# The first matrix of an MLP by Strassen's scheme, its results through DRAM

## The chip, the cores and the metric

The kernel is one program on one core of a Trainium2 chip. The metric is the device time of one execution in microseconds (us). Engines are called as in the profile: PE (TensorE, the matrix multiplier), DVE (VectorE), ACT (ScalarE), POOL (GpSimd) and SP (SyncE, which issues the DMAs here). A matrix product accumulates in a PSUM bank; a bank holds 128 x 512 values of 32 bits, and there are eight, called bank0 to bank7.

## The reference

Two blocks of a network run one after the other on 1024 tokens of 1024 channels. The change touches the last stage, the MLP of the second block, whose hidden layer is 4096 wide:

```python
def squared_relu_mlp(x, w1, w2):
    hdn = jnp.square(jax.nn.relu(jnp.einsum('bld,df->blf', x, w1.astype(jnp.float32))))
    return jnp.einsum('blf,fd->bld', hdn, w2.astype(jnp.float32))
...
        h = layer_norm_2(ALPHA * h + cross_attention(...), ln2_g[l], ln2_b[l])
        h = layer_norm_2(ALPHA * h + squared_relu_mlp(h, mlp_w1[l], mlp_w2[l]), ln3_g[l], ln3_b[l])
```

Everything is in fp32. `layer_norm_2` subtracts the mean of a token's channels and divides by the root of their variance (plus 1e-5), then applies a gain and a bias.

## The kernel before, in words

P is 128, D and T (channels and tokens) are 1024, HALF is 512, KD is 8. Channels lie on the partitions: the activations are held per half of the tokens (`self.h[hf]`, hf 0 or 1) as 128 x 8 x 512, part k being channels 128k to 128k+127.

**Products of fp32 matrices.** The matmuls take operands of type fp32r, and every operand x is split into two of them: hi, x cast to fp32r, and lo, x - hi. `split` (L165) does that with a cast on ACT (L166) and a subtraction on DVE (L167); `wload` (L139) loads a block of weights of 128 x 1024 into a tile `wraw` and splits it likewise into `whi` (ACT, L149) and `wlo` (DVE, L150). `mm3` (L153) then issues three matmuls for each 128 x 128 piece of weights and 512 tokens: hi x hi (L157), hi x lo (L158), lo x hi (L159). So a product over all 1024 channels takes 8 x 3 = 24 matmuls into one bank.

**The MLP.** `mlp` (L1904) goes through the hidden layer in eight steps, fb = 0 to 7, of 512 hidden channels. In a step, the first matrix runs over four weight blocks of 128 hidden channels, each times two halves of the tokens: eight groups of 24 matmuls, the activations (`act[hf]`, tiles ahi and alo of each half) being the moving operand. The sink of each group applies ReLU from the bank (ACT, L1914), squares it (DVE, L1915), and splits the result into a pair of x4 tiles, the operand `fa` of the second matrix. Then four blocks of the second matrix run, each as four groups of 12 matmuls, and each group is added to `h` (L1935 in step 0, L1937 after). The last step ends in `mlp_last` (L1939), which computes the last part of the second matrix with the operands exchanged, a token block at a time, normalizes and stores it. In step 0 the first matrix goes through `gemm_lag`, which starts a block's first half of the tokens two blocks ahead of its second half, because the second half of the activations comes later: it is the normalization of `norm_ln` (L1857 to L1860), in front of the MLP.

**What sets the order.** The kernel is written as a plain sequence; a tile scheduler orders each engine's instructions by a simulated timeline and by priorities. `early(...)` raises the priority of what is issued in it, as the weight loads and the sinks are. Within an engine instructions run in the order that came out, and each waits for the semaphores of what it reads or overwrites. SP issues the DMAs in the same way. Tiles come from pools with a fixed number of buffers to a tag: three each for wraw, whi and wlo (L1057), four each for x40 and x41, seven for x2, three each for y20 and y21 (L1802 to L1810). A tile of a tag can only be written when the tile that had its buffer has been read for the last time. PSUM banks are dealt in rings (L95): mm is banks 0 and 1.

## Time and profile before

| what | value |
|---|---|
| time, median of 3 runs | 3163.79 us (3158.67 to 3164.6) |
| profiled execution, its own time | 3173.28 us |
| span of that execution | 3171.5 us |
| mean granted clock of PE | 0.964 |
| PE busy | 97% of the span, 15504 matmuls |
| weight loads of PE (PEld) busy | 79% |
| DVE busy | 59% |
| ACT busy | 30% |
| POOL busy | 9% |

The span runs from the first to the last instruction of the profiled execution; its own time holds a little more around it. Durations that the trace gives are those of this one execution. Matmuls are pipelined: their recorded durations overlap, so what one costs PE is the distance of the starts of two in a row. The granted clock is the share of full clock at which PE was allowed to run: 1.00 is 2.4 GHz, 0.50 is 1.2 GHz. The MLP runs from about 2424 us (first matmuls of step 0) to the end at 3171.5.

### The profile page before, as it was taken

What the parts mean: (1) busy time and instruction counts of PE and PEld (TensorE: products, weight loads), DVE (VectorE), ACT (ScalarE), POOL (GpSimd) and SP (SyncE); (2) the same over time, 40 slices, a digit from 0 to 9 for tenths busy, and PEclk for the clock granted to TensorE, in tenths of its full rate; (3) what the DMA queues carried; (4) which work ended last, traced back from release to release, by engine and by line L of the source; (5) the groups of instructions that cost most, each with busy time, mean ns of one, the idle gap of its engine ahead of it and who ended that gap; (6) DMA issues with size and microseconds to landing.
All of it is one profiled execution on the core that took longest, in us unless ns stands there. A gap on an engine that the chain in (4) does not pass through costs nothing.

```text
span 3171.5 us, 40262 instructions
## 1 busy us (share of the span) xinstructions
PE 3061.3 (97%) x15504; PEld 2521.2 (79%) x15504; DVE 1871.1 (59%) x3884; ACT 955.0 (30%) x1650; POOL 273.0 (9%) x761
## 2 busy tenths in 40 slices
PE   8999899999989999999999899889999999999998
PEld 7978788787867887878788787778787888888887
DVE  4987657564856455564665679886456333333336
ACT  3323434343432121221243235433334111222212
POOL 0000222221085000000000000210000000000000
PEclk8999889887999999999999999999999999999999
DMA  4123444435422111121211543423021111111111
GB/s 158 52 95 107 146 109 126 114 85 155 144 64 61 51 47 57 51 61 47 73 55 47 147 137 100 127 70 110 37 87 50 54 54 47 47 47 47 47 47 54
DMA packets 193137, 254.62 MB, mean 80 GB/s; under 512 B 45745, under 2 KB 136753, under 8 KB 192433
## 3 DMA queue, kind: packets, MB, share of 16 engines
q1 hardware_dynamic: 192944, 252.05, 26.0%
q8 instruction: 122, 2.00, 0.3%
q14 instruction: 71, 0.57, 0.1%
HBM read 195.11 MB, written 57.93 MB: 80 GB/s over the span
## 4 chain that ended last, share of the span: by engine, by line
PE 84%; DVE 6%; DMA 4%; POOL 3%; issue 1%; ACT 1%; SPq 0%; ACTq 0%; DVEq 0%; POOLq 0%
PE bank L157 22%; PE bank L159 22%; PE bank L158 22%; PE bank L161 2%; PE bank L162 2%; PE bank L163 2%; PE bank L751 1%; PE bank L752 1%; DVE zt L1348 1%; PE bank L197 1%; PE bank L322 1%; DMA ix<-scr 1%; DMA zx<-zt 1%; PE bank L775 1%; PE bank L588 1%
## 5 line engine op out<-in xcount | busy, mean ns | idle before, releaser
L157 PE MATMUL bank<-ahi,whi 128*128 128x512 f32 x1856 | 743.2, 401 | 13.0 <-DVE zt L1288 4.7
L159 PE MATMUL bank<-ahi,wlo 128*128 128x512 f32 x1856 | 740.4, 399 | 0.0
L158 PE MATMUL bank<-alo,whi 128*128 128x512 f32 x1856 | 737.8, 398 | 1.1 <-DVE alo L167 1.1
L149 ACT CAST whi<-wraw 128x1024 fp32r<-128x1024 f32 (+1 forms) x242 | 253.6, 1049 | 842.9 <-PE bank L158 759.0
L157 PEld LDWEIGHTS bank<-ahi,whi 128*128 128x128 f32 x1856 | 351.3, 189 | 93.0 <-issue 6.3
L159 PEld LDWEIGHTS bank<-ahi,wlo 128*128 128x128 f32 x1856 | 354.5, 191 | 86.4 <-issue 2.1
L158 PEld LDWEIGHTS bank<-alo,whi 128*128 128x128 f32 x1856 | 351.1, 189 | 87.7 <-issue 2.7
L150 DVE TENSOR_TENSOR wlo<-wraw,whi 128x1024 fp32r<-128x1024 f32 (+1 forms) x242 | 297.3, 1229 | 166.6 <-ACT whi L149 153.4
L159 PE MATMUL bank<-x,wlo 128*128 128x512 f32 x448 | 177.9, 397 | 0.0
L158 PE MATMUL bank<-x,whi 128*128 128x512 f32 x448 | 177.1, 395 | 0.0
L157 PE MATMUL bank<-x,whi 128*128 128x512 f32 x448 | 175.4, 392 | 0.0
L1937 DVE TENSOR_TENSOR h<-h,bank 128x512 f32<-128x512 f32 x96 | 66.0, 688 | 161.0 <-PE bank L159 160.3
L157 PE MATMUL bank<-fhi,whi 128*128 128x512 f32 x352 | 139.6, 397 | 10.0 <-DVE h L1159 10.0
L158 PE MATMUL bank<-flo,whi 128*128 128x512 f32 x352 | 140.0, 398 | 0.0
L157 PE MATMUL bank<-hi,whi 128*128 128x512 f32 x320 | 130.0, 407 | 10.1 <-ACT hi L272 9.2
L159 PE MATMUL bank<-fhi,wlo 128*128 128x512 f32 x352 | 139.7, 399 | 0.0
L1159 DVE TENSOR_TENSOR h<-h,bank 128x512 f32<-128x512 f32 x96 | 65.5, 686 | 114.0 <-PE bank L159 113.9
L159 PE MATMUL bank<-hi,wlo 128*128 128x512 f32 x320 | 131.2, 410 | 0.0
L158 PE MATMUL bank<-lo,whi 128*128 128x512 f32 x320 | 130.3, 407 | 0.0
L1915 DVE TENSOR_TENSOR y<-y 128x512 f32<-128x512 f32 x64 | 44.0, 689 | 103.5 <-ACT y L1914 103.5
L157 PEld LDWEIGHTS bank<-x,whi 128*128 128x128 f32 x448 | 84.8, 189 | 19.9
L158 PEld LDWEIGHTS bank<-x,whi 128*128 128x128 f32 x448 | 84.1, 188 | 20.6
(766 smaller groups left out, 5539.8 us busy)
## 6 DMA issues: line engine op xcount, KB each, us to landing
wraw<-in_w_m_dram SPq DMA_DIRECT2D x60, 512.0 KB, 3.6
wraw<-in_w_o_dram SPq DMA_DIRECT2D x24, 512.0 KB, 4.2
wraw<-in_w_fg_dram SPq DMA_DIRECT2D x22, 512.0 KB, 3.5
wraw<-in_w_fu_dram SPq DMA_DIRECT2D x22, 512.0 KB, 3.6
wraw<-in_w_fd_dram SPq DMA_DIRECT2D x22, 512.0 KB, 3.5
hd<-h SPq DMA_DIRECT2D x4, 2048.0 KB, 6.8
s5m<-s5m SPq DMA_DIRECT2D x8, 896.0 KB, 4.7
x<-in_xT_dram SPq DMA_DIRECT2D x8, 512.0 KB, 10.1
```

The source lines that it names most:

```text
L149: nc.scalar.copy(hi[:, :n], raw[:, :n])
L150: nc.vector.tensor_sub(lo[:, :n], raw[:, :n], hi[:, :n].bitcast(F32))
L157: mm(ps, lhsT=wh, rhs=xh, start=first, stop=False)
L158: mm(ps, lhsT=wh, rhs=xl, start=False, stop=False)
L159: mm(ps, lhsT=wl, rhs=xh, start=False, stop=last)
L161: mm(ps, lhsT=xh, rhs=wh, start=first, stop=False)
L162: mm(ps, lhsT=xh, rhs=wl, start=False, stop=False)
L163: mm(ps, lhsT=xl, rhs=wh, start=False, stop=last)
L197: self.nc.tensor.matmul(ps[:, i:i + 1], lhsT=x[:, i * P:(i + 1) * P], rhs=self.k("ones")[:, 0:1], start=j == 0, stop=j == len(xs) - 1)
L1159: V.tensor_add(h, h, ps)
L1915: V.tensor_mul(x, x, x)
L1937: V.tensor_add(self.h[hf][:, d], self.h[hf][:, d], ps)
```

## The change

**What it computes.** The last 28 of the 32 weight blocks of the first matrix are taken in 14 pairs (n, n+1). Halves of channels (K, parts 0 to 3 and 4 to 7) are called L and R. With A11 = W[n] L, A12 = W[n] R, A21 = W[n+1] L, A22 = W[n+1] R, and for the activations B11, B21 = parts 0 to 3 and 4 to 7 of the first half of the tokens, B12, B22 = those of the second half, the four results of a pair (two blocks, two halves of tokens) come from seven products over half the channels each, in the Winograd form of Strassen's scheme. The order is: 1 (A11 with B11), 6 (A21 + A22 - A11 with t2), 5 (A21 + A22 with t1), 7 (A11 - A21 with t3), 2 (A12 with B21), 3 (A12 - (A21 + A22 - A11) with B22), 4 (A22 with t4), where t1 = B12 - B11, t2 = B22 - t1, t3 = B22 - B12 and t4 = B21 - t2. In the code u = t2 is computed as v + B11 with v = t3 and t4 as B21 - B11 - t3, the same sums. Each product is 4 parts x 3 = 12 matmuls into one bank (ring "fast", six banks).

**Operands** (`fast_operands`). The sums of the activations are formed once, from the fp32 values in `h`, on DVE (L1920, L1922, L1923) and POOL, and split. t2 and t3 fill all eight x4 tiles, t4 lies in six x2 tiles and two tiles of another pool, and t1 overwrites parts 0 to 3 of `act[1]`, that is B12, which no product uses by itself.

**Weights** (`fast_pairs`). A generator loads both raw blocks of a pair, forms the sums of its halves on POOL (four additions of 128 x 512 a pair) and splits each of the seven left operands into one of six slots (halves of the three whi and three wlo tiles). Six are made ahead; each product then takes the next one and asks for one more.

**Results.** ACT copies the first product out of its bank (m1), DVE adds the others as they come (L1990 to L2011, seven additions a pair), ReLU and square follow as before, and each 128 x 512 result is sent to a DRAM scratch tensor `fd[n]` (2 MB a step of four blocks). The first four blocks run as before through `gemm_lag` with their 24 matmuls and go to `fd` too. After all of the first matrix, the second matrix runs through its eight steps: each loads its four blocks from `fd` into the x4 tiles (now as raw fp32) and splits them into `act[fb % 2]`, which is no longer needed for the activations; the matmuls, the additions to `h` and `mlp_last` are as before.

```diff
--- before.py
+++ after.py
@@ -93,7 +93,7 @@
 
 
     RINGS = {"mm": "01", "l1": "4567", "s": "23", "cf": "45", "ar": "23", "ad": "4", "inv": "56", "cr": "7", "cd": "1", "ho": "2", "kv": "0", "kv0": "017", "wo": "04",
-             "s5": "34567", "s5m": "67", "dn": "0145", "ml": "234567", "rg": "2", "sa": "34", "sb": "562", "so": "7", "sc": "0123", "tp": "67"}
+             "s5": "34567", "s5m": "67", "dn": "0145", "ml": "234567", "rg": "2", "sa": "34", "sb": "562", "so": "7", "sc": "0123", "tp": "67", "fast": "234567"}
 
     def psum(self, kind):
         banks = self.RINGS[kind]
@@ -1901,23 +1901,136 @@
                         self.split(ah[:, 4:8, ls], al[:, 4:8, ls], pt)
         self.gemm_lag(self.vwd, self.act, self.ln_sink("ln2_g", "ln2_b"), 5, 3)
 
+    def fast_operands(self):
+
+        V, G = self.nc.vector, self.nc.gpsimd
+
+        def halves(tiles):
+            return [v[:, o:o + HALF] for v in tiles for o in (0, HALF)]
+        t2, t3 = ([halves([self.x4(z) for _ in range(2)]) for z in range(2)] for _ in range(2))
+        t4 = [[self.x2(dt=F32R) for _ in range(3)] + [self.t(self.rp, [P, HALF], f"rb{z}", F32R)] for z in range(2)]
+        h0, h1 = self.h
+        b11, b21, t1, b22 = ([[self.act[hf][z][:, o + k] for k in range(4)] for z in range(2)] for hf in range(2) for o in (0, 4))
+
+        for k in range(4):
+            v, u, w = (self.y2(1) for _ in range(3))
+            V.tensor_sub(v, h1[:, 4 + k], h1[:, k])
+            G.tensor_tensor(u, v, h0[:, k], op=ALU.add)
+            V.tensor_sub(w, h0[:, 4 + k], h0[:, k])
+            V.tensor_sub(w, w, v)
+            for t, x in ((t3, v), (t2, u), (t4, w)):
+                self.split(t[0][k], t[1][k], x)
+        for k in range(4):
+            u = self.y2(1)
+            G.tensor_tensor(u, h1[:, k], h0[:, k], op=ALU.subtract)
+            self.split(t1[0][k], t1[1][k], u)
+        return {1: b11, 2: b21, 3: b22, 4: t4, 5: t1, 6: t2, 7: t3}
+
+    def fast_pairs(self, srcs, ops, sink):
+
+        nc = self.nc
+        V, A, G = nc.vector, nc.scalar, nc.gpsimd
+        his, los = ([self.t(self.wp, [P, 1056], z, F32R) for _ in range(3)] for z in ("whi", "wlo"))
+        slots = [(his[j][:, o:o + HALF], los[j][:, o:o + HALF]) for j in range(3) for o in (0, HALF)]
+        at = [0]
+
+        def part(x):
+            s = slots[at[0] % 6]
+            at[0] += 1
+            self.split(s[0], s[1], x)
+            return s
+
+        L, R = slice(0, HALF), slice(HALF, 2 * HALF)
+
+        def weights():
+
+            for n in range(0, len(srcs), 2):
+                r0, r1, s = (self.t(self.wp, [P, 1056], "wraw") for _ in range(3))
+                for r, src in ((r0, srcs[n]), (r1, srcs[n + 1])):
+                    nc.sync.dma_start(r[:, :D], src)
+                yield part(r0[:, L])
+                G.tensor_tensor(s[:, L], r1[:, L], r1[:, R], op=ALU.add)
+                G.tensor_tensor(s[:, R], s[:, L], r0[:, L], op=ALU.subtract)
+                yield part(s[:, R])
+                yield part(s[:, L])
+                G.tensor_tensor(r1[:, L], r0[:, L], r1[:, L], op=ALU.subtract)
+                yield part(r1[:, L])
+                yield part(r0[:, R])
+                G.tensor_tensor(r0[:, R], r0[:, R], s[:, R], op=ALU.subtract)
+                yield part(r0[:, R])
+                yield part(r1[:, R])
+        made, todo = weights(), []
+
+        def more():
+            with self.early():
+                w = next(made, None)
+            if w:
+                todo.append(w)
+        for _ in range(6):
+            more()
+
+        def prod(m):
+            ps = self.psum("fast")
+            wh, wl = (v.rearrange("p (k n) -> p k n", k=4) for v in todo.pop(0))
+            for k in range(4):
+                self.mm3(ps, wh[:, k], wl[:, k], ops[m][0][k], ops[m][1][k], k == 0, k == 3)
+            more()
+            return ps
+        for n in range(0, len(srcs), 2):
+            p = prod(1)
+            with self.early(100000):
+                m1 = self.y2(0)
+                A.copy(m1, p)
+            p = prod(6)
+            with self.early(100000):
+                u = self.y2(1)
+                V.tensor_add(u, m1, p)
+            p5 = prod(5)
+            with self.early(100000):
+                v = self.y2(1)
+                V.tensor_add(v, u, p5)
+            p = prod(7)
+            with self.early(100000):
+                V.tensor_add(u, u, p)
+                x = self.x2()
+                V.tensor_add(x, u, p5)
+                sink(n + 1, 1, x)
+            p = prod(2)
+            with self.early(100000):
+                V.tensor_add(m1, m1, p)
+                sink(n, 0, m1)
+            p = prod(3)
+            with self.early(100000):
+                V.tensor_add(v, v, p)
+                sink(n, 1, v)
+            p = prod(4)
+            with self.early(100000):
+                V.tensor_add(u, u, p)
+                sink(n + 1, 0, u)
+
     def mlp(self):
         nc, tc = self.nc, self.tc
         V, A, PE = nc.vector, nc.scalar, nc.tensor
+
+        def sink(n, hf, ps, x=None):
+            x = self.y2(0) if x is None else x
+            A.activation(x, ps, AF.Relu)
+            V.tensor_mul(x, x, x)
+            nc.sync.dma_start(self.fd[n][:, hf * HALF:(hf + 1) * HALF], x)
+        self.gemm_lag(self.a["w_m1"][0:4], self.act, sink, 2, 0)
+        ops = self.fast_operands()
+        self.fast_pairs([self.a["w_m1"][n] for n in range(4, 32)], ops, lambda n, hf, x: sink(4 + n, hf, x, x))
+
         for fb in range(8):
-            fa = []
-            for i in range(4):
-                fa.append((self.x4(0), self.x4(1)))
-            def sink(n, hf, ps, fa=fa):
-                sl = slice(hf * HALF, (hf + 1) * HALF)
-                x = self.y2(1)
-                A.activation(x, ps, AF.Relu)
-                V.tensor_mul(x, x, x)
-                self.split(fa[n][0][:, sl], fa[n][1][:, sl], x)
-            if fb == 0:
-                self.gemm_lag(self.a["w_m1"][0:4], self.act, sink, 2, 0)
-            else:
-                self.gemm_group([self.a["w_m1"][4 * fb + i] for i in range(4)], self.act, sink, group=2)
+            fa = [tuple(v[:, 2 * i:2 * i + 2].rearrange("p z t -> p (z t)") for v in self.act[fb % 2]) for i in range(4)]
+            with self.early(100000):
+                for i in range(4):
+                    x = self.t(self.lp, [P, T], f"x4{i % 2}", bufs=4)
+                    nc.sync.dma_start(x, self.fd[4 * fb + i])
+                    self.split(fa[i][0], fa[i][1], x)
             if fb == 7:
                 return self.mlp_last(fa)
             for u in range(4):
@@ -1997,6 +2110,7 @@
                   ("s5m", [P, 16, 7 * P]), ("s5t", [16, 16, 2 * P])):
         setattr(e, n, e.t(e.dram, sh, n))
     e.od = [e.t(e.dram, [8, P, HALF], f"od{hf}") for hf in range(2)]
+    e.fd = [e.t(e.dram, [P, T], f"fd{n}") for n in range(4 * D // P)]
     e.dt = e.t(e.cp, [P, 8, 8], "dt")
     e.s5_r8 = e.t(e.cp, [P, 16], "s5r8")
```

**Where instructions move: DVE, start of the MLP.** Before, DVE's rows behind the last normalization of the second half of the tokens (L1858 adds a row sum to all 8 parts of h1; `alo1` is the low part of its activations; y21 tiles are results of the first weight blocks and x40, x41 the operand of the second matrix):

```order
L1858 TENSOR_TENSOR h1_1511_7613<-h1_1511_7613,x2_3457_20211 128x512 x8
L167 TENSOR_TENSOR alo1_1510_7612<-h1_1511_7613,ahi1_1509_7611 128x512 x8
L150 TENSOR_TENSOR wlo_3494_20450<-wraw_3492_20447,whi_3493_20449 128x1024
L1915 TENSOR_TENSOR y21_3491_20442<-y21_3491_20442 128x512
L167 TENSOR_TENSOR x41_3468_20302<-y21_3491_20442,x40_3467_20301 128x512
L150 TENSOR_TENSOR wlo_3505_20576<-wraw_3503_20573,whi_3504_20575 128x1024
L1915 TENSOR_TENSOR y21_3496_20478<-y21_3496_20478 128x512
```

After, the piece that ends the operand sums, 32 rows behind the same L1858 rows (x40_3528 and x41_3530 hold t2, x40_3532 and x41_3534 t3, x2 and rb tiles t4; alo1 is now t1's low part, wlo a slot of the pairs):

```order
L167 TENSOR_TENSOR x41_3534_20596<-y21_3552_20644,x40_3532_20594 128x512
L167 TENSOR_TENSOR wlo_3562_20676<-wraw_3567_20681,whi_3559_20673 128x512
L1923 TENSOR_TENSOR y21_3554_20646<-y21_3554_20646,y21_3552_20644 128x512
L167 TENSOR_TENSOR x41_3530_20592<-y21_3553_20645,x40_3528_20590 128x512
L167 TENSOR_TENSOR rb1_3542_20604<-y21_3554_20646,rb0_3538_20600 128x512
L2021 TENSOR_TENSOR y20_3520_20498<-y20_3520_20498 128x512
L2021 TENSOR_TENSOR y20_3522_20527<-y20_3522_20527 128x512
L2021 TENSOR_TENSOR y20_3524_20556<-y20_3524_20556 128x512
L167 TENSOR_TENSOR alo1_1542_7644<-y21_3555_20657,ahi1_1541_7643 128x512
L167 TENSOR_TENSOR alo1_1542_7644<-y21_3556_20661,ahi1_1541_7643 128x512
L167 TENSOR_TENSOR alo1_1542_7644<-y21_3557_20665,ahi1_1541_7643 128x512
L167 TENSOR_TENSOR wlo_3564_20678<-wraw_3565_20679,whi_3561_20675 128x512
```

What moved: between the normalization and the splits into the operands of the products stand the sums of the activations, their splits, the first weight slots; the four splits of t1 come last, behind three squares (L2021, before L1915) of the first four blocks.

**DVE within the first matrix.** Before, in step fb = 1, DVE's rows are one square and one split of each result, and the splits of the next weights:

```order
L1915 TENSOR_TENSOR y21_3546_20866<-y21_3546_20866 128x512
L167 TENSOR_TENSOR x41_3532_20822<-y21_3546_20866,x40_3531_20821 128x512
L1915 TENSOR_TENSOR y21_3548_20896<-y21_3548_20896 128x512
L167 TENSOR_TENSOR x41_3534_20824<-y21_3548_20896,x40_3533_20823 128x512
L150 TENSOR_TENSOR wlo_3558_20970<-wraw_3556_20967,whi_3557_20969 128x1024
L1915 TENSOR_TENSOR y21_3550_20926<-y21_3550_20926 128x512
L167 TENSOR_TENSOR x41_3532_20822<-y21_3550_20926,x40_3531_20821 128x512
L150 TENSOR_TENSOR wlo_3569_21096<-wraw_3567_21093,whi_3568_21095 128x1024
```

After, one of the 14 pairs (bank tiles are the products, y20 and y21 the running sums m1, u and v; wraw holds a raw block, or its sums):

```order
L1990 TENSOR_TENSOR y21_3588_20875<-y20_3583_20853,bank4_3584_20855 128x512
L167 TENSOR_TENSOR wlo_3563_20677<-wraw_3585_20868,whi_3560_20674 128x512
L1994 TENSOR_TENSOR y21_3590_20894<-y21_3588_20875,bank5_3589_20877 128x512
L167 TENSOR_TENSOR wlo_3563_20677<-wraw_3587_20870,whi_3560_20674 128x512
L1997 TENSOR_TENSOR y21_3588_20875<-y21_3588_20875,bank6_3591_20896 128x512
L167 TENSOR_TENSOR wlo_3564_20678<-wraw_3587_20870,whi_3561_20675 128x512
L1999 TENSOR_TENSOR x2_3592_20912<-y21_3588_20875,bank5_3589_20877 128x512
L2003 TENSOR_TENSOR y20_3583_20853<-y20_3583_20853,bank7_3593_20917 128x512
L2021 TENSOR_TENSOR x2_3592_20912<-x2_3592_20912 128x512
L167 TENSOR_TENSOR wlo_3564_20678<-wraw_3586_20869,whi_3561_20675 128x512
L2021 TENSOR_TENSOR y20_3583_20853<-y20_3583_20853 128x512
L2007 TENSOR_TENSOR y21_3590_20894<-y21_3590_20894,bank2_3594_20937 128x512
```

What moved: no result is split here any more, the additions of products come in, and the weight splits are half as wide and seven to a pair instead of two of full width.

**PE at a border of two groups.** Before, in step fb = 1, the first half of the tokens, from block 0 to block 1 (whi and wlo are the weights, ahi0 and alo0 the activations of the first half):

```order
L158 MATMUL bank0_3545_20841<-alo0_1507_7606,whi_3540_20831 128x512
L159 MATMUL bank0_3545_20841<-ahi0_1506_7605,wlo_3541_20832 128x512
L157 MATMUL bank1_3547_20871<-ahi0_1506_7605,whi_3543_20837 128x512
L158 MATMUL bank1_3547_20871<-alo0_1507_7606,whi_3543_20837 128x512
L159 MATMUL bank1_3547_20871<-ahi0_1506_7605,wlo_3544_20838 128x512
```

After, in a pair, from product 1 to product 6 (x40 and x41 hold t2):

```order
L158 MATMUL bank3_3582_20838<-alo0_1539_7638,whi_3559_20673 128x512
L159 MATMUL bank3_3582_20838<-ahi0_1538_7637,wlo_3562_20676 128x512
L157 MATMUL bank4_3584_20855<-x40_3527_20589,whi_3560_20674 128x512
L158 MATMUL bank4_3584_20855<-x41_3529_20591,whi_3560_20674 128x512
L159 MATMUL bank4_3584_20855<-x40_3527_20589,wlo_3563_20677 128x512
```

What moved: a group has 12 matmuls instead of 24, the moving operand changes between groups, and bank follows bank in a ring of six instead of two.

## Rows read from the trace of the kernel before

**Rows 1.** Page, part 1: busy time, share of the span, instructions.
```profile
span 3171.5 us, 40262 instructions
...
PE 3061.3 (97%) x15504; PEld 2521.2 (79%) x15504; DVE 1871.1 (59%) x3884; ACT 955.0 (30%) x1650; POOL 273.0 (9%) x761
```

**Rows 2.** Windows of the MLP: stretch, us, busy (x instructions), clock, DMA share, GB/s.
```profile
2430.00:2446.00 16.00, 10.14 (x50) 7.76 (x49) 14.18 (x34) 6.77 (x11) 0.00 (x0) 0.89 0.07 17
2446.00:2470.00 24.00, 24.00 (x97) 19.43 (x98) 8.70 (x13) 9.46 (x16) 0.00 (x0) 0.93 0.15 44
2470.00:2512.00 42.00, 42.00 (x182) 33.98 (x182) 19.22 (x25) 8.11 (x11) 0.00 (x0) 1.00 0.17 52
2567.00:2657.00 90.00, 90.00 (x389) 72.73 (x388) 31.98 (x41) 18.33 (x25) 0.00 (x0) 1.00 0.15 48
2657.00:2747.00 90.00, 90.00 (x388) 72.83 (x387) 32.00 (x42) 17.76 (x25) 0.00 (x0) 1.00 0.15 48
```

**Rows 3.** Timeline of PE: start, us, line, operation, operands.
```profile
2449.84 0.39 PE L159 MATMUL bank<-ahi,wlo 128*128 128x512 f32 x1
...
2452.37 0.39 PE L159 MATMUL bank<-ahi,wlo 128*128 128x512 f32 x1
...
2656.03 0.39 PE L159 MATMUL bank<-x,wlo 128*128 128x512 f32 x1
...
2675.63 0.39 PE L159 MATMUL bank<-x,wlo 128*128 128x512 f32 x1
```

**Rows 4.** MLP (2404 to 3172), groups by line: busy, mean ns | idle before.
```profile
L150 DVE TENSOR_TENSOR wlo<-wraw,whi 128x1024 fp32r<-128x1024 f32 x62 | 76.0, 1225 | 98.3 <-ACT whi L149 98.1
L1937 DVE TENSOR_TENSOR h<-h,bank 128x512 f32<-128x512 f32 x96 | 66.0, 688 | 161.0 <-PE bank L159 160.3
L149 ACT CAST whi<-wraw 128x1024 fp32r<-128x1024 f32 x62 | 65.1, 1051 | 348.3 <-PE bank L158 348.3
L167 DVE TENSOR_TENSOR x<-y,x 128x512 fp32r<-128x512 f32 x64 | 44.1, 692 | 36.6 <-ACT x L166 36.6
L1915 DVE TENSOR_TENSOR y<-y 128x512 f32<-128x512 f32 x64 | 44.0, 689 | 103.5 <-ACT y L1914 103.5
L166 ACT CAST x<-y 128x512 fp32r<-128x512 f32 x64 | 39.6, 621 | 66.2 <-DVE y L1915 66.2
L1914 ACT ACTIVATE y<-bank 128x512 f32<-128x512 f32 x64 | 38.0, 595 | 117.5 <-PE bank L159 117.5
```

**Rows 5.** Chain of waits behind the normalization: start, us, engine, what, line.
```profile
2440.30 4.90 DVE h L1858 x8
...
2445.86 0.79 PE bank L158
2446.65 0.43 PE bank L159
...
2449.21 0.33 PE bank L159
```

**Rows 6.** Timeline of POOL in the SSD stage.
```profile
2036.51 2.71 POOL L1752 TENSOR_TENSOR sdxe<-sdxd,h 128x512 f32<-128x512 f32 x1 [2.27 <-PE bank L1778]
...
2046.86 1.04 POOL L1779 TENSOR_TENSOR sdprev<-sdprev,h 128x512 f32<-128x512 f32 x1 [2.47 <-PE bank L1772]
```

**Rows 7.** Timeline of DVE in the SSD stage.
```profile
2046.95 1.50 DVE L1783 TENSOR_TENSOR sdy<-sdy,sdzc 128x512 f32<-128x512 f32 x1
...
2059.68 0.67 DVE L1783 TENSOR_TENSOR sdy<-sdy,sdzc 128x512 f32<-128x512 f32 x1
```

**Rows 8.** Page, part 6: DMA issues, KB each, median us to landing.
```profile
wraw<-in_w_m_dram SPq DMA_DIRECT2D x60, 512.0 KB, 3.6
...
hd<-h SPq DMA_DIRECT2D x4, 2048.0 KB, 6.8
```

**Rows 9.** Tile view of the weight blocks of the first matrix.
```profile
DMA to landing us min/median/max: 3.5/3.6/4.7
```

**Rows 10.** Waits in the MLP: us in total, times, longest us.
```profile
ACT whi L149 <- PE bank L158: 348.3, 58, 10.2
...
PE bank L157 <- ACT ahi L166: 3.5, 1, 3.5
```

## Prediction

> **What bounds the kernel now.** I read the busy table first: PE is busy for 97% of the span, and no other engine for more than 59% [rows 1]. Then the windows of the MLP, stage by stage. From 2470 us on PE is busy for the whole of every window, at a granted clock of 1.00, while DVE is busy for about a third of it; only 2430 to 2446, where the normalization of the second half of the tokens runs, has a hole, with the clock down in it [rows 2]. So in the MLP a matmul that goes takes its time with it, if nothing new makes PE wait.
>
> What one matmul is worth is not its duration. The groups of matmuls have means near 399 ns, but consecutive ones overlap: the timeline gives starts 19.60 us apart for 84 matmuls, 0.2333 us each [rows 3]. Two windows of 90 us hold 389 and 388 records, 0.231 and 0.232 us each [rows 2]. I take 0.232.
>
> By the Trainium skill ("TensorE: Matmul & The Clock Gate", section "Wait — 56ns, not 53.3ns?") matmuls of 512 columns start 215.7 ns apart at full clock. The trace does not agree (233 ns), and the measurement decides; by the page the matmul term below would be 36.2 us.
>
> **Part 1, fewer matmuls.** A pair of weight blocks took 2 blocks x 2 halves of tokens x 24 = 96 matmuls. Now it is 7 products x 4 parts of K x 3 = 84. The 28 blocks after the first four are 14 pairs: 14 x 12 = 168 matmuls go, all in a stretch where PE has no idle. 168 x 0.232 = 39.0 us. The first four blocks, the second matrix and the last block keep their counts. The order shows products of 12 matmuls, one bank each, one behind the other; groups of 12 are what the second matrix runs already, at the pitch of [rows 3] and without gaps, so shorter groups cost nothing.
>
> **Part 2, what is added beside PE in a pair.** PE needs 84 x 0.232 = 19.5 us per pair (22.3 before).
> - DVE: 7 half-wide weight splits, 7 additions that read a bank and 4 squares, 18 instructions of 128x512 where there were 4 squares, 4 activation splits and 2 weight splits. One is 0.69 us by duration and 0.61 by pitch (eight in 4.90 us) [rows 4, 5]: 18 x 0.61 = 11.0 us. Fits.
> - ACT: 7 casts, 1 copy, 4 ReLUs, about 0.62 us each [rows 4]: 7.4 us. Fits.
> - POOL, which has nothing in the MLP now: 4 additions of two SBUF operands. The same shape took from 1.04 to 2.71 us in the SSD stage [rows 6]: 4.2 to 10.8 us. Fits.
> - DVE beside POOL: with a POOL addition running, a DVE instruction with two SBUF inputs took 1.50 us, and the same line took 0.67 without [rows 7]. So they keep each other out. Added up without overlap, 11.0 + 4.2 = 15.2 us of 19.5, and PE stays the bound. The Trainium skill ("GPSIMD Engine Reference", section "Key points") says that GpSimd shares its SBUF interfaces with VectorE and contends with instructions that have two SBUF inputs; by this rule 11 of the 18 contend (splits and squares), and it is the source of the second rival below.
> - DMA: two weight blocks in and four half-blocks of 256 KB out per pair, 2 MB in 19.5 us, about 107 GB/s; a weight block lands in 3.6 us, and 2 MB went out in 6.8 us [rows 8], some 300 GB/s. Fits.
>
> The weight parts run up to five products ahead (six slots), 5 x 12 x 0.232 = 13.9 us. The tightest stretch: a pair's second raw block is loaded only when the last part of the pair before is split, some 4.3 us into a pair (one product of 2.8, a cast, a subtraction). It lands 3.6 us later; two POOL additions of 1.04, a cast and a subtraction bring the first part that needs it to 4.3 + 3.6 + 2.1 + 1.3 = 11.3 us. PE wants it after 8 products, at 22.3. With POOL at 2.71 it is 14.6. Slack of 8 to 11 us, so I cost the steady state at nothing. What hides it is those five products; without the cover each pair would pay the difference, as in the first rival.
>
> **Part 3, the start of the products.** The operand sums are formed while PE works off the four plain blocks. Those end near 2475: PE has 15 matmuls at the low pitch of 0.43 us behind the hole [rows 5] and then about 105 at 0.232. DVE is behind its normalization at 2445.2 [rows 5], and the order puts 36 instructions (24 of the sums and their splits, the 8 activation splits, 4 of weights) there before the last split of the sums: 36 x 0.61 + 0.6 for the wide weight split = 22.6, to 2468; beside them 7 POOL additions that can each hold DVE up for 1.04: to 2475. The second product needs its operand (t2) from 2475 + 2.8, its last quarter 2.1 later. It fits with 3 to 5 us. The third product's operand (t1) overwrites the activations that the last plain block reads, so it can't start before 2475; its first cast and subtraction end 1.3 us later, its fourth some 4 us later, and PE wants them from 2480.6. In front of them on ACT, in order, stand three ReLUs, and on DVE three squares. I take a stall of 1.5 us. Bounds: 0 if nothing is late; if each of the 7 POOL additions takes 2.71, DVE ends at 2487 and PE waits 9 us, and another 15 matmuls run at 0.43 instead of 0.232, 3 us more.
>
> **Part 4, the seam to the second matrix and the end.** The results go out to DRAM and come back as the operand of the second matrix. The first read waits for the t2 tiles, free after the last pair's second product, and five products (13.9 us) are left then. Load 3.6, cast 1.05, subtraction 1.23 [rows 4, 8]: the first operand is there at 6, the fourth at some 13 us (the tiles that it goes into come free by then). I take 1 us; bounds 0, and 5 if the five transfers queue at 3.6 each. In the second matrix DVE has, per 192 matmuls (44.5 us), 4 operand splits and 4 weight splits of 1.23 and 16 additions of 0.69: 20.8 us. It fits. Block 8's first weights now wait for the last plain use of the other activation tile (before, they were early); split 2.3 us, other matmuls behind that use about 4 us: nothing, at most 2. Below nothing: some runs of matmuls show 0.230 us (eleven in 2.53) [rows 3]; if the 1344 of the second matrix got this for reading other tiles, 4.4 us would be gained. No row says why they should, so I leave it out.
>
> **Sum.** 39.0 - 1.5 - 1.0 = 36.5 us. The profiled execution took 3173.3 (span 3171.5 and 1.8 around it): 3136.8. It stands 9.5 above the median of the runs shown, 3163.8; the same difference there gives 3127.3, say 3127.
>
> **Rivals.**
> 1. *Slower: the loop of the weights sets the pace.* The next pair's raw block waits for the last part of this one, so load, sums and splits are one loop around a pair. With each step at its longest row and none overlapped: load 4.7 [rows 9], three POOL additions at 2.71, seven parts with a cast of 0.62 and a subtraction of 1.50: 4.7 + 8.1 + 14.8 = 27.6 us per pair against 22.3 before, 14 x 5.3 = 74 us slower, 3240. For: ACT's longest waits in the MLP are those before a weight cast [rows 10], and all of it is in-order. Against: with usual rows it is 3.6 + 3.1 + 7 x 1.3 = 15.8, and casts and subtractions overlap. It takes something from 19.5 us on, and makes the kernel slower from 22.3 + 2.6 / 14 less the stalls, about 22.1.
> 2. *DVE becomes the bound through POOL.* If every one of the 11 contending instructions took 1.50: 11 x 1.50 + 7 x 0.69 = 21.3 us per pair, a gain of 1.0 x 14 = 14 less 2.5: 3152. For: [rows 7]. Against: only 4 POOL additions per pair, which can hold up 4, not 11.
> 3. *Start and seam cost their bounds.* 39.0 - 9 - 3 - 5 - 2 = 20: 3144. For: t1 has no slack by construction. Against: POOL took 1.04 in most rows of its stage.
> 4. *The matmuls are there, but not the gain*: PE at lower clock. Only holes lower it here [rows 2, 5], and none of some length is added. Part of 3.
>
> **How the numbers follow.** Forecast 0.73 (its own range 3117 to 3141: all bounds at nothing and the 4.4 gained, less 3 for the runs' spread of 6 us; or 9 and 5 lost). Start and seam 0.11, DVE 0.08, loop 0.06, of the rest nothing clear. The range of 8 in 10 reaches to rivals 3 and, almost, 2: 3117 to 3150. A measurement can't tell 0.2% (6.3 us) from no change here: faster ends at 3157.5. Forecast, rival 3, most of 2 and some of 1's mild forms: 0.89 faster; 0.04 same; 0.07 slower.
>
> **What would show it.** PE with 15336 matmuls, pitch 0.232 in the products and hardly an idle group. Right on part 2: ACT's weight casts wait for PE (slots), not for POOL or DMA; POOL's additions between 1.04 and 2.71; DVE under 80% busy. Part 3: a wait of PE for ACT or DVE writing t1 or t2, under 3 us. Part 4: none over 2 us at the seam. Wrong: PE idle regularly in each pair, behind a weight split (rival 1) or behind a bank that DVE has not read (rival 2), or a pitch over 0.24 us with no waits, which nothing here expects.

## The result and the profile after

The changed kernel takes 3130.82 us (median of 7 runs, 3121.05 to 3148.84) against 3163.79 (7 runs, 3158.67 to 3177.79): a ratio of 0.9888, 95% interval 0.9856 to 0.9919, that is 26 to 46 us less. The forecast was 3127.

The two profiled executions lie further apart, 49.3 us by span. The page of the changed kernel, part 1:

```profile
span 3122.2 us, 40749 instructions
...
PE 3010.8 (96%) x15336; PEld 2479.1 (79%) x15336; DVE 1986.7 (64%) x4048; ACT 992.6 (32%) x1718; POOL 371.3 (12%) x825
```

168 matmuls fewer, and PE is still the engine that is always busy. But not all of the 49.3 us is the change's. Both kernels run the same instructions in the same order up to the MLP, and yet the last normalization began at 2440.30 before [rows 5] and at 2421.09 after (chain of waits: start, us):

```profile
2421.09 4.91 DVE h L1858 x8
```

Most of these 19 us are one stretch in which the clock was granted low. Windows of the same piece of work, from one DVE instruction to the 96th behind it (the columns are those of [rows 2]), of before, of the changed kernel, and of the changed kernel profiled once more:

```profile
606.65:662.11 55.46, 54.92 (x350) 46.20 (x351) 29.74 (x96) 15.60 (x41) 13.84 (x36) 0.63 0.25 66
```

```profile
599.96:637.69 37.73, 37.20 (x350) 31.96 (x351) 30.59 (x97) 15.62 (x41) 13.56 (x36) 1.00 0.37 97
```

```profile
596.69:649.32 52.63, 52.47 (x354) 44.67 (x353) 29.80 (x97) 15.63 (x41) 13.59 (x36) 0.68 0.26 70
```

The same instructions took 55.5 us at a granted clock of 0.63, and 37.7 at 1.00, 17.7 less, and one and the same kernel took 37.7 once and 52.6 the other time. PE was busy for nearly all of each window; why the clock was low, no run here shows. Total times spread accordingly: over 19 us in the seven runs of the kernel before, over 28 in those of the changed one, whose fastest (3121) had a mean granted clock of 0.969 and whose slowest (3149) 0.960. I therefore read the effect from the **MLP stage**: from the first of the eight row-sum additions of the last normalization (L1858) to the end of the span. It took 3171.5 - 2440.3 = 731.2 before and 3122.2 - 2421.1 = 701.1 after: 30.0 us less. The changed kernel, profiled once more without an edit, gave 703.4 (below), so this stage came out 2.3 us apart in two profiles of one kernel.

Windows of the changed kernel: the start of the products, the middle of the pairs, and two of the seam between the two matrices:

```profile
2456.00:2464.00 8.00, 6.40 (x29) 4.87 (x28) 7.92 (x9) 4.36 (x8) 5.08 (x4) 1.00 0.15 57
2530.00:2620.00 90.00, 90.00 (x389) 72.80 (x388) 57.48 (x87) 33.52 (x59) 28.20 (x20) 1.00 0.35 110
2736.00:2742.00 6.00, 3.28 (x14) 2.35 (x14) 6.00 (x8) 2.00 (x3) 0.00 (x0) 1.00 1.03 401
2742.00:2750.00 8.00, 8.00 (x29) 6.33 (x29) 2.78 (x4) 1.02 (x1) 0.00 (x0) 0.79 1.04 414
```

In the pairs PE never idles, as before [rows 2], while DVE has gone from 32 to 57 of 90 us. The start has 1.6 us of idle PE, the seam 2.7, and behind the seam the clock is at 0.79. All waits of PE from the anchor on (us in total, times, longest):

```profile
PE bank L158 <- DVE alo L167: 3.6, 4, 1.6
PE bank L157 <- ACT ahi L166: 3.5, 1, 3.5
PE bank L157 <- DVE h L2048: 2.7, 1, 2.7
```

The wait for ahi is the hole of the normalization, there before [rows 10]; of the first row, 1.1 us lies there too. New are the three waits for alo (t1) at the start, 2.5 us (the window above ends behind the first), and the one for h at the seam, 2.7.

### The profile page after: what moved, and what is told of

Read it like the earlier page. It is cut to its first block, busy times and chain, and to the rows that moved or that the text cites. A ratio compares the mean times of both kernels' runs of the same rounds, so it can differ in the third digit from the quotient of the medians.

```text
span 3122.2 us, 40749 instructions
## 1 busy us (share of the span) xinstructions
PE 3010.8 (96%) x15336; PEld 2479.1 (79%) x15336; DVE 1986.7 (64%) x4048; ACT 992.6 (32%) x1718; POOL 371.3 (12%) x825
## 4 chain that ended last, share of the span: by engine, by line
PE 83%; DVE 6%; DMA 5%; POOL 4%; issue 2%; ACT 1%; SPq 0%; ACTq 0%; DVEq 0%; POOLq 0%
PE bank L157 22%; PE bank L159 22%; PE bank L158 21%; PE bank L161 2%; PE bank L162 2%; PE bank L163 2%; PE bank L751 1%; PE bank L197 1%; PE bank L752 1%; PE bank L322 1%; PE bank L188 1%; DMA ix<-scr 1%; POOL ixl L574 1%; DMA wraw<-in_w_q_dram 1%; PE bank L775 1%
## 5 line engine op out<-in xcount | busy, mean ns | idle before, releaser
L157 PE MATMUL bank<-ahi,whi 128*128 128x512 f32 x2080 | 834.5, 402 | 15.7 <-DVE zt L1288 4.7
L158 PE MATMUL bank<-alo,whi 128*128 128x512 f32 x2080 | 826.9, 398 | 3.6 <-DVE alo L167 3.6
L159 PE MATMUL bank<-ahi,wlo 128*128 128x512 f32 x2080 | 830.0, 399 | 0.0
L159 PEld LDWEIGHTS bank<-ahi,wlo 128*128 128x128 f32 x2080 | 397.7, 191 | 97.1 <-issue 2.1
L167 DVE TENSOR_TENSOR wlo<-wraw,whi 128x512 fp32r<-128x512 f32 x98 | 74.7, 765 | 61.0 <-ACT whi L166 61.0
L166 ACT CAST whi<-wraw 128x512 fp32r<-128x512 f32 x98 | 59.8, 617 | 124.2 <-POOL wraw L1956 53.8
L157 PEld LDWEIGHTS bank<-fhi,whi 128*128 128x128 f32 x352 | 67.0, 190 | 27.0 <-DVE h L1159 10.6
L157 PEld LDWEIGHTS bank<-hi,whi 128*128 128x128 f32 x320 | 62.9, 197 | 25.0 <-ACT hi L272 8.9
L158 PEld LDWEIGHTS bank<-flo,whi 128*128 128x128 f32 x352 | 66.7, 190 | 16.1
L159 PEld LDWEIGHTS bank<-fhi,wlo 128*128 128x128 f32 x352 | 66.6, 189 | 15.3
```

Of the source, the lines that this page charges most:

```text
L157: mm(ps, lhsT=wh, rhs=xh, start=first, stop=False)
L158: mm(ps, lhsT=wh, rhs=xl, start=False, stop=False)
L159: mm(ps, lhsT=wl, rhs=xh, start=False, stop=last)
L166: self.nc.scalar.copy(hi, x)
L167: self.nc.vector.tensor_sub(lo, x, hi.bitcast(F32))
```

## Experiments

Each is an edit of the changed kernel; the stage is read from its profile.

**Only the way through DRAM**

```diff
-        ops = self.fast_operands()
-        self.fast_pairs([self.a["w_m1"][n] for n in range(4, 32)], ops, lambda n, hf, x: sink(4 + n, hf, x, x))
+        self.gemm_group([self.a["w_m1"][n] for n in range(4, 32)], self.act, lambda n, hf, ps: sink(4 + n, hf, ps), group=2)
```

> All 32 blocks of the first matrix run as 24-matmul groups, as before the change; only the way of the results (to DRAM, back, all of the first matrix ahead of the second) is kept. Measured by the MLP stage of the profile: from the first of the eight row-sum additions of the last normalization to the end of the span; 731.2 us before, 701.1 after. Theory (the gain is the 168 matmuls, the DRAM way costs a wait of PE at the seam): 15504 matmuls, stage 731 to 736, same time as before within 0.3%. Rival A (the new arrangement, with one switch between the matrices instead of fourteen, gives part of the gain): stage under 728. Rival B (the DRAM way costs more than the seam shows, and products give back more): stage over 739.

Stage 732.8 (731.2 before), time 3164.2 against 3163.9, ratio 1.0002 (0.9967 to 1.0036). PE has no wait at the seam. The trip through DRAM and the new arrangement neither cost nor give anything that shows; the gain is the products'.

**One product of seven left out**

```diff
-            p = prod(3)
-            with self.early(100000):
-                V.tensor_add(v, v, p)
+            todo.pop(0)
+            more()
+            with self.early(100000):
                 sink(n, 1, v)
```

> Left out: the 12 matmuls of product 3 of each pair and the addition of its bank; all seven weight parts are still formed and their slots taken. Theory (PE's pitch of 0.233 sets a pair's time, everything else has slack): 168 matmuls less, stage 701.1 - 39.2 = 662, and PE still without waits in the pairs. Rival (the loop of load, POOL sums and splits is close behind PE): a pair of six products needs 16.8 us of PE; if the loop takes about 18, the stage falls by 20 only (681), with PE waiting for weight splits in every pair.

Stage 667.0, 34.1 less than the changed kernel; time 3094.1, 37 less. From 2480 on PE has no wait before the seam, and a pair takes 16.75 us, 6 x 12 x 0.233. The stage missed its 662 by 5. Of that, 3.4 lie in longer waits at the two ends (1.3 us instead of 0.23 from one matmul to the next at 2478, for a weight part, and 5.5 instead of 3.1 at the seam) and 0.8 in more matmuls at the low clock behind the seam; the rest is less than two profiles of one kernel differ by. So a matmul of the pairs is worth its pitch, even with a seventh less of them.

**What stands behind PE**

```diff
-                self.mm3(ps, wh[:, k], wl[:, k], ops[m][0][k], ops[m][1][k], k == 0, k == 3)
+                nc.tensor.matmul(ps, lhsT=wh[:, k], rhs=ops[m][0][k], start=k == 0, stop=k == 3)
```

> Left out: two of the three matmuls of every piece in the products (hi x lo and lo x hi), so that a pair needs 28 matmuls, 6.5 us of PE. Everything else of a pair stays, so the pairs now run at the pace of what stands behind PE, and 14 pairs show it. Forecast of the prediction for the loop of the weights with usual rows: 15.8 us a pair; the products then take 14 x 15.8 = 221 us instead of 274, stage about 648. Rival 1 of the prediction with its longest rows: 27.6 us a pair, stage over 800. Rival 2 (DVE through POOL): 21.3 a pair, stage about 725, DVE without idle.

Stage 632.1. A pair in the middle takes 14.3 us: nine of them lie between these two additions (13.98 to 14.83 each; the 14.0 of the next expectation is that of the shortest, and low by 0.3):

```profile
2503.93 0.67 DVE L1994 TENSOR_TENSOR y<-y,bank 128x512 f32<-128x512 f32 x1
...
2632.63 0.67 DVE L1994 TENSOR_TENSOR y<-y,bank 128x512 f32<-128x512 f32 x1
```

Window of the middle:

```profile
2530.00:2620.00 90.00, 55.77 (x169) 38.60 (x168) 88.53 (x117) 40.13 (x72) 40.11 (x24) 0.76 0.45 154
```

DVE is busy for 88.5 of 90. PE's own waits in the pairs are all for weight casts, which by themselves would point at the loop of the weights:

```profile
PE bank L1979 <- ACT whi L166: 57.1, 21, 5.2
```

But that loop passes through DVE's splits, and DVE itself waits for a cast for only 2.2 of 160 us: DVE is the next bound. DVE's groups there (2500 to 2660; busy us, mean ns of one):

```profile
L167 DVE TENSOR_TENSOR wlo<-wraw,whi 128x512 fp32r<-128x512 f32 x78 | 69.3, 913 | 2.3 <-ACT whi L166 2.2
L2021 DVE TENSOR_TENSOR y<-y 128x512 f32<-128x512 f32 x33 | 37.8, 1158 | 1.2 <-ACT y L2020 1.2
...
L1994 DVE TENSOR_TENSOR y<-y,bank 128x512 f32<-128x512 f32 x11 | 7.4, 676 | 0.1
```

18 instructions at a pitch of 0.60 would be 10.8 us. Of the other 3.5, 3.1 are instructions with two SBUF inputs that ran beside a POOL addition (913 and 1158 ns in the mean, against 678), the rest is idle. Those that read a bank kept 0.67, also the 20 that ran beside a POOL addition between 2500 and 2660.

**The same with the weight sums on DVE.** In `weights()` four lines change alike:

```diff
-                G.tensor_tensor(s[:, L], r1[:, L], r1[:, R], op=ALU.add)
+                V.tensor_tensor(s[:, L], r1[:, L], r1[:, R], op=ALU.add)
```

> As the kernel with a third of the products (left out: the hi x lo and lo x hi matmuls of the products), and the four additions of weight halves a pair on DVE instead of POOL. With the third alone, the pairs went at about 14.0 us in the middle, DVE busy for 88.5 of 90, with instructions of 0.68 that took up to 1.78 beside POOL. Theory (the two keep each other out, so that the four additions on POOL cost DVE 14.0 - 18 x 0.60 = 3.2 us a pair, more than the 2.4 that they take on DVE): a pair takes 22 x 0.60 = 13.2, stage 632.1 - 14 x 0.8 = 621. Rival A (POOL does relieve DVE): a pair takes 14.5 or more, stage 639 or more. Rival B (the loop of loads and splits is as close as DVE): no change within 3 us.

Stage 622.2, a pair 13.6 us (nine between these two rows), DVE as full:

```profile
2489.98 0.67 DVE L1994 TENSOR_TENSOR y<-y,bank 128x512 f32<-128x512 f32 x1
...
2612.47 0.68 DVE L1994 TENSOR_TENSOR y<-y,bank 128x512 f32<-128x512 f32 x1
```

```profile
2530.00:2620.00 90.00, 63.67 (x183) 45.35 (x184) 87.43 (x145) 47.25 (x81) 0.00 (x0) 0.73 0.45 155
```

The pairs are faster by 0.7 us with four instructions more on DVE, and 14 x 0.7 = 9.8 is what the stage fell by (9.9). On POOL the four additions took 6.8 us of POOL and, with DVE's idle time, 3.5 of DVE; on DVE itself they take some 2.8.

**The weight sums on DVE, all products** (the four lines above alone)

> The four additions of weight halves a pair run on DVE instead of POOL. Theory (nothing beside PE sets the pace in the pairs): stage 701 within 2; DVE busy for about 57.5 of 90 us still, as 4 more instructions a pair (4 x 0.61 = 2.4 us of 19.5) stand against DVE instructions that no longer lengthen under POOL: none of 128x512 over 0.8 us in the pairs. Rival (DVE's instructions are not lengthened by POOL, so DVE rises by 11 us per 90; PE may wait for it): DVE 68 of 90, stage 701 to 715.

Stage 704.4, time 3130.9: no gain, no loss that the stage can tell, as PE sets the pace. But I was wrong on DVE, whose busy time rises:

```profile
2530.00:2620.00 90.00, 90.00 (x389) 72.81 (x388) 66.03 (x105) 33.84 (x55) 0.00 (x0) 1.00 0.31 100
```

66 against 57.5. No instruction of 128x512 takes over 0.7 us there, as expected; but POOL had lengthened few in the changed kernel. Between 2500 and 2660, 18 instructions with two SBUF inputs ran beside a POOL addition in it, at 0.88 us in the mean; with DVE full they were 60, at 1.25. What POOL costs depends on how full DVE is.

**Product 5 later** (order 1, 6, 7, 2, 5, 3, 4; the weights in that order too)

```diff
-            p5 = prod(5)
-            with self.early(100000):
-                v = self.y2(1)
-                V.tensor_add(v, u, p5)
             p = prod(7)
             with self.early(100000):
-                V.tensor_add(u, u, p)
-                x = self.x2()
-                V.tensor_add(x, u, p5)
-                sink(n + 1, 1, x)
+                v, u = u, self.y2(1)
+                V.tensor_add(u, v, p)
...
+            p = prod(5)
+            with self.early(100000):
+                V.tensor_add(v, v, p)
+                x = self.x2()
+                V.tensor_add(x, u, p)
+                sink(n + 1, 1, x)
```

> The products of every pair run in the order 1, 6, 7, 2, 5, 3, 4, so that t1 is wanted two products (5.6 us) later. In the changed kernel PE waited four times for t1's low parts at the start, 3.6 us in all; the last one was split at 2467.3 and PE had wanted the first at 2462. Theory (t1 has no slack because product 5 stands third): with 5.6 us more the waits go, stage 701.1 - 3.6 = 697.5, within 1.5. Rival (DVE and POOL are behind by more than that, and t2, t3 or the first weight parts are late in its place): PE waits 2 us or more elsewhere in the first pair, stage 700 or more.

Stage 700.1, PE's waits:

```profile
PE bank L157 <- DVE h L2048: 4.6, 1, 4.6
...
PE bank L158 <- DVE alo L167: 1.1, 1, 1.1
PE bank L159 <- DVE wlo L167: 0.4, 1, 0.4
```

The waits for t1 are gone (0.4 is left, for a weight part), but the wait for the bank at the seam has grown from 2.7 to 4.6. So the stage moved by 1 where 3.6 were expected, which is less than two profiles of one kernel differ by, and only the place of the waits answers the question. Part of the longer wait at the seam may be chance: the changed kernel without an edit had 2.7 there in one profile and 3.6 in the other.

**The activation sums on DVE** (two lines of `fast_operands`)

```diff
-            G.tensor_tensor(u, v, h0[:, k], op=ALU.add)
+            V.tensor_tensor(u, v, h0[:, k], op=ALU.add)
...
-            G.tensor_tensor(u, h1[:, k], h0[:, k], op=ALU.subtract)
+            V.tensor_tensor(u, h1[:, k], h0[:, k], op=ALU.subtract)
```

> The eight additions of the activation sums that ran on POOL (four for t2, four for t1) run on DVE; the order of the products is that of the changed kernel. There POOL took 1.67 us for each of t1's, and beside POOL single DVE instructions took 1.78 us in place of 0.68. Theory A (the start is late because of the order of the products: t1 may be written only when the last plain block has read the activations): the wait for the first part stays (1 us or more), the three others shrink; waits 1.5 to 3 us, stage 699 to 701. Theory B (it is POOL that makes t1 late): all four waits go, stage 697.5. Rival (DVE is short of time at the start): more waiting than 3.6 us, stage over 702.

Stage 698.7, and no wait for t1 at all; what is left of the alo row is the normalization's 1.1:

```profile
PE bank L157 <- DVE h L2048: 3.8, 1, 3.8
...
PE bank L158 <- DVE alo L167: 1.1, 1, 1.1
```

Theory B: POOL made t1 late. One thing more changed in this run (and in the run below that adds eight banks to it): in the first pair the scheduler put the last six matmuls of product 5 between and behind those of product 7. But the first six stood where they had, and the longest wait, 1.6 us, had been among them; and the last part of t1 was split by 2472.7, some 0.3 us before the old order would have wanted it. (With product 5 late the waits go too: t1 comes late only measured against the moment at which it is wanted.) In the changed kernel POOL's rows at the start are

```profile
2447.11 1.63 POOL L1959 TENSOR_TENSOR wraw<-wraw,wraw 128x512 f32<-128x512 f32 x1
...
2457.09 5.00 POOL L1928 TENSOR_TENSOR y<-h,h 128x512 f32<-128x512 f32 x3 [3.73 <-DVE y L1923]
2463.91 1.68 POOL L1928 TENSOR_TENSOR y<-h,h 128x512 f32<-128x512 f32 x1 [1.83 <-DVE alo L167]
```

(the row of 5.00 is three additions), and DVE beside and without POOL:

```profile
2447.51 1.78 DVE L167 TENSOR_TENSOR x<-y,x 128x512 fp32r<-128x512 f32 x1
...
2455.03 0.68 DVE L167 TENSOR_TENSOR x<-y,x 128x512 fp32r<-128x512 f32 x1
...
2459.14 4.09 DVE L2021 TENSOR_TENSOR y<-y 128x512 f32<-128x512 f32 x3
```

Three additions of 1.67 in a row, which began only at 2457.09 because of a wait for DVE, and the fourth at 2463.91, waiting for a buffer. Beside them the three squares that stand before t1's first split took 4.09 us on DVE, where three alone take 1.9 (pitch 0.60). With the edit, DVE forms t1's sums in 0.68 each:

```profile
2464.22 0.68 DVE L1928 TENSOR_TENSOR y<-h,h 128x512 f32<-128x512 f32 x1
```

**All eight banks for the second matrix** (a new ring `m2`, "01234567", beside those of L95)

```diff
-                        ps = self.psum("mm")
+                        ps = self.psum("m2")
```

> The second matrix goes round all eight banks in place of two; the order of DVE's instructions stays the same. In the changed kernel PE waited 2.7 us for an addition to h (that frees one of the two banks) which stands on DVE behind the splits of the next step's operand, and then ran 11 matmuls at the lower clock, 2 us more. Theory (DVE's queue at the seam is the wait, the data were there): the wait and the low clock go, stage 701.1 - 4.8 = 696.3, within 1.5. Rival (the data from DRAM, or the weights of the second matrix, come as late as the additions): PE waits as long for a split, stage 699 to 701.

Stage 696.6, 4.5 less; no wait at the seam and no low clock behind it (a window across the seam):

```profile
PE bank L158 <- DVE alo L167: 3.6, 4, 1.6
PE bank L157 <- ACT ahi L166: 3.5, 1, 3.5
```

```profile
2745.00:2755.00 10.00, 10.00 (x44) 8.12 (x43) 10.00 (x13) 4.32 (x6) 0.00 (x0) 1.00 1.04 407
```

The operands were there. DVE's instructions come in the same order up to the first addition to h, and with more banks PE goes on.

**Both ends: product 5 late, and eight banks** (the two edits above together)

> Product 5 late and eight banks together. Theory: both waits go, stage 701.1 - 3.6 - 4.8 = 692.7, within 2; time 8 us less than that of the changed kernel, about 1.22% less than the kernel before's (ratio 0.986 to 0.989). Rival (the waits hide others of the same size): stage 697 or more, ratio as of the changed kernel.

Stage 693.7, time 3120.7, ratio 0.9880 (0.9849 to 0.9911).

**Both ends: activation sums on DVE, and eight banks** (likewise)

> The activation sums on DVE and the second matrix round eight banks; the order of the products is that of the changed kernel. Theory: neither wait is left, PE waits in the MLP only at the normalization as before the change; stage 701.1 - 2.9 - 4.5 = 693.7, within 1.5, as with product 5 late. Rival (the sums cost DVE time that the seam or the first pair lacks): a wait of PE over 1 us in the first pair or at the seam, stage 695 or more.

Stage 692.4, time 3114.1 (5 runs, 3112.8 to 3137.7), ratio 0.9874 (0.9839 to 0.9910): by its median and by the stage ahead of both kernels, though its interval in total time overlaps that of the changed kernel. PE's waits are those of the normalization:

```profile
PE bank L157 <- ACT ahi L166: 3.5, 1, 3.5
...
PE bank L158 <- DVE alo L167: 1.1, 1, 1.1
```

**The changed kernel again**

> The changed kernel once more, without any edit, as a measure of how far the stage repeats: 701.1 within 1.5, with the same waits (t1 at the start, the bank at the seam). If it differs by more than 3, the differences of the other kernels' stages under 3 us tell nothing.

Stage 703.4, time 3131.3: 2.3 more than the first profile, outside what I had allowed, inside what I had called readable. Waits of 2.7 for t1 and 3.6 for the bank: the two ends, with the low clock behind them, take 10.4 us there and 7.8 in the first profile (PE's starts, over the pitch), which is the difference of the stages. So the ends are what does not repeat, and the single steps of 1 to 5 us above are less sure than the two runs that take both waits away.

## Why the prediction was right, and where its steps were not

**Part 1 held.** With both new waits taken away the stage is 731.2 - 692.4 = 38.8 us shorter than before; forecast for the matmuls 39.0. Leaving out a further product took 34.1 and longer waits at the ends. The pairs ran at 233 ns a matmul.

**Part 2: the sign held, the bound behind PE was misplaced.** PE does not idle in the pairs. I had taken the loop of load, sums and splits as the dangerous one (15.8 us a pair, slack 8 to 11); without PE in the way the pairs ran at 14.3, with DVE full. My sum for DVE and POOL end to end, 15.2, was the right term, but that it came so close is in part luck: POOL's four additions took 6.8 us, not 4.2, and of these only about half (3.5) fell on DVE. Also wrong: "ACT's weight casts wait for PE (slots), not for POOL or DMA". They waited 81 us for POOL's sums and 17 for loads, against 25 for PE:

```profile
ACT whi L166 <- POOL wraw L1956: 53.8, 13, 5.0
...
ACT whi L166 <- POOL wraw L1962: 26.2, 14, 1.9
ACT whi L166 <- PE bank L158: 25.0, 23, 1.7
```

No harm came of it in the pairs, where PE never waits; the casts run up to five products ahead. The durations of POOL's weight sums, 1.32 to 1.79 in the mean, lay in the lower half of my bounds (groups of the MLP: busy us, mean ns, idle before):

```profile
L167 DVE TENSOR_TENSOR wlo<-wraw,whi 128x512 fp32r<-128x512 f32 x98 | 74.7, 765 | 61.0 <-ACT whi L166 61.0
...
L1962 POOL TENSOR_TENSOR wraw<-wraw,wraw 128x512 f32<-128x512 f32 x14 | 25.1, 1791 | 87.3 <-DVE wlo L167 87.3
...
L1955 POOL TENSOR_TENSOR wraw<-wraw 128x512 f32<-128x512 f32 x14 | 18.5, 1319 | 87.8 <-DMA wraw<-in_w_m_dram 72.3 <-DVE wlo L167 13.2 <-DVE wlo L150 2.4
```

Not so the four additions for t2 at the start, at 2.26 us in the mean; the longest was beyond my upper bound of 2.71, while DVE beside it kept its pace of 0.60:

```profile
2435.00 3.48 POOL L1921 TENSOR_TENSOR y<-y,h 128x512 f32<-128x512 f32 x1 [4.84 <-DVE x L167]
```

The Trainium skill ("GPSIMD Engine Reference", section "Key points") has GpSimd contend with VectorE instructions that have two SBUF inputs. The runs agree: 0.68 became 1.78 us beside a POOL addition, while additions with a bank as one input stayed at 0.67.

**Part 3: right place, wrong reason, too small.** Forecast a stall of 1.5 because t1 can be written only after the last plain block, with three squares ahead; measured 2.5 us of waiting, 3.0 between matmuls:

```profile
2463.89 0.50 PE L158 MATMUL bank<-alo,whi 128*128 128x512 f32 x1 [1.60 <-DVE alo L167]
...
2466.19 0.50 PE L158 MATMUL bank<-alo,whi 128*128 128x512 f32 x1 [0.65 <-DVE alo L167]
...
2467.40 0.50 PE L158 MATMUL bank<-alo,whi 128*128 128x512 f32 x1 [0.24 <-DVE alo L167]
```

All of it goes when the sums leave POOL. The dependence that I named was met in time: the last plain block ended at about 2456.3, a product ahead of the second one's start, and t1's first cast ran at 2458.92. The step that failed is costing POOL's additions at 1.04 there: they took 1.67 and more, and the three squares that I had counted in front of t1's splits took 4.09 us beside them. (The 15 matmuls at the low pitch were also misread: 11 ran so before the change, 3 in front of the wait for alo and 8 behind it. In the changed kernel they were 15.)

**Part 4: wrong mechanism, too small.** Forecast 1 for a late first operand. PE's rows at the seam:

```profile
2738.61 0.40 PE L159 MATMUL bank<-ahi,wlo 128*128 128x512 f32 x1
2741.73 0.51 PE L157 MATMUL bank<-ahi,whi 128*128 128x512 f32 x1 [2.72 <-DVE h L2048]
...
2743.01 0.63 PE L158 MATMUL bank<-alo,whi 128*128 128x512 f32 x1
```

It had run two groups, so the operand was there, and as forecast (the four splits of it ended from 2724.9 to 2732.9, 6 to 13 us behind the last pair's second product); the third group waited 2.7 us for an addition to h to free one of two banks, and of the next dozen most started 0.43 us apart, 1.7 us more in all. The sign that I had named, no wait over 2 us at the seam, did not hold. DVE's rows tell why:

```profile
2735.78 0.68 DVE L2011 TENSOR_TENSOR y<-y,bank 128x512 f32<-128x512 f32 x1
2736.38 2.36 DVE L167 TENSOR_TENSOR alo<-x,ahi 128x1024 fp32r<-128x1024 f32 x2
2738.65 0.69 DVE L2021 TENSOR_TENSOR y<-y 128x512 f32<-128x512 f32 x1
2739.26 1.22 DVE L150 TENSOR_TENSOR wlo<-wraw,whi 128x1024 fp32r<-128x1024 f32 x1
2740.39 0.68 DVE L2021 TENSOR_TENSOR y<-y 128x512 f32<-128x512 f32 x1
2740.99 0.68 DVE L2048 SCALAR_TENSOR_TENSOR h<-h,bank 128x512 f32<-128x512 f32 x1
```

Two splits of the next step's operand (the row of 2.36), a weight split and two squares ran ahead of the first addition (L2048), whose bank was complete a whole group, 2.8 us, before PE stopped. I had counted DVE's time per step, which fits, and not what stood in its queue at the change of steps.

**The sum.** Forecast 39.0 - 1.5 - 1.0 = 36.5. In the stage: 39.2 (168 x 0.2333), less 3.0 and 2.9 between matmuls at the two ends, less 1.7 for the low clock behind the seam and 0.8 for four matmuls more at low clock behind the normalization = 30.8; measured 30.0 (27.8 for the second profile). The two ends cost 7.6 where 2.5 was forecast. These 5 us are less than the spread of the runs: that the median came within 4 us of the forecast does not show that the ends were right, and in the stage the forecast was off by 6.5 and 8.7. Rivals 1 and 2 are excluded by the full PE in the pairs; rival 3 was right in kind, with 7.6 of the 19 us that it gave these ends. Rival 4, for which the sum had no term, is there as the 1.7 and the 0.8: the new hole at the seam did lower the clock behind it.

## What to carry to other kernels

Where an engine is busy without gaps, instructions taken off it are worth their pitch, and what is left to predict is the ends: the first operands, and the switch to the next phase, where an in-order queue still holds the old phase's last work and the next phase's early work. Two banks were enough for the second matrix at every place but that switch. And an addition of two SBUF inputs moved from DVE to POOL cost DVE more than it relieved it once DVE was full (14.3 against 13.6 us a pair); leave it on DVE unless DVE has time to spare and POOL's result is not waited for.

## What the runs showed of the hardware

The lengthening goes both ways: the first weight sum of a pair on POOL took 1.32 us in the mean in the changed kernel, and 1.66 where DVE was full. And it shows on DVE the more, the busier DVE is: 0.77 us for a weight split in the mean of the changed kernel, 0.91 there.
